# One offset for layer 1's weight halves, eight-wide inverse roots on GpSimd, and a planner with other costs

## The chip, the cores and the metric

The kernel runs on one core of a Trainium2 chip. The metric is device time in microseconds (us) of one execution; before the change the median of three runs is 1524.97 us (1524.93 to 1526.73). All numbers are float32; products run in the `float32r` form of TensorE unless said otherwise.

## The reference

Two layers over 256 latent and 256 context tokens of width 1024. Cut to what matters:

```python
for l in range(2):
    mod = silu(c) @ w_mod[l] + b_mod[l]           # and the same for c_ctx
    h = rms_norm(x, norm1_g[l]) * (1 + sc1) + sh1
    z = h @ w_in[l]                               # 14 column groups
    y_da  = differential attention, heads rms-normed before and after
    y_gla = chunked gated linear attention, both directions, rms-normed heads
    y_na  = 2-D neighbourhood attention
    m = sum over the three of sigmoid(gate) * (y @ w_br)
    x = x + g1 * (m @ w_out)
    h2 = rms_norm(x, norm2_g[l]) * (1 + sc2) + sh2
    x = x + g2 * (relu(h2 @ w_ff1) ** 2 @ w_ff2)
```

In layer 0 latent and context tokens go through everything (512 columns). In layer 1 the context only feeds keys, values and states, so most products have 256 columns. Every `rms_norm` needs `1 / sqrt(mean + eps)`: of 2 or 4 values per partition for the layer norms and the attention's output heads, of 8 for the linear attention's heads, of 16 or 32 for queries and keys. The linear attention's decay needs `gla_a2`, `gla_a_b` (in the kernel one array, `gl`: the gate factors) and triangular matrices (`tri`).

## The kernel before, in words

**Weights.** All weights stream once, as 290 pieces of 128 x 1024 float32 (512 KB, `raw`, 5 buffers), 145 a layer, over SP's DMA queue. Each piece is split into a rounded half and a rest: ScalarE copies it into `wh`, VectorE subtracts into `wl` (128 x 1152 tiles of which 1024 columns are used, 5 buffers each). A product is three matmuls: `wh` with the high half of the data, `wh` with the low half, `wl` with the high half. In `tok_job` (the token-major projections) the weights are the moving operand and 512 wide; in `chan_mm` (gates, branches, output projection, both MLP products) the weights are the stationary operand, 128 x 128, and the data moves, 512 columns in layer 0 and 256 in layer 1.

**Where a piece lies.** A `wh` or `wl` tile is 1152 x 4 = 4608 bytes, nine times 512, per partition. Pieces of layer 0 and of the token-major projections start at its begin. Layer 1's other pieces are planned with `shift=True`; `split_weights` takes their columns from an offset that depends on the place in the turn of five:

```python
SHIFTS = 16, 48, 64, 80, 112
i = SHIFTS[st["ring"]] if plan[n][1] else 0
st["ring"] = (st["ring"] + 1) % NW
h, lo = [buf(t, t, 1152, NW, F32R)[:, i:i + 1024] for t in ("wh", "wl")]
```

These are 64, 192, 256, 320 and 448 bytes. Piece n, counted from 0, has place n mod 5; the last one, 289, has place 4.

**The order of the work.** It is written by a planner while the program is built. Generators (the stream of projections `stream`, `branches` with the three attentions, `norms`, `mods_task`, `begin`) yield a time at which they could go on; `drive` takes the next that is ready, or the earliest. Times come from `Plan.note`, which adds up costs per engine from the tables `FIXED`, `PER`, `SLOWER`, `SWITCH` and `LATENCY`. `refill` adds a split of a piece when the planned time of its load has come. `copy` and `square` choose ScalarE or VectorE by `act_first`. Each engine then runs its own queue strictly in the order written, so an instruction that waits holds back all behind it on that engine.

**Inverse roots.** `rsqrt` is a seed from the bits and three Newton steps, all on VectorE: a scaling with eps, one seed, and 9 small instructions. `norm_rms` (6 calls) runs it for the layer norms and copies the result into `rb`, which TensorE broadcasts (`norm_bcast`); `heads_rms` runs it for queries and keys (8 calls on 16 or 32 values) and for the linear attention (3 on 8 values); `head_end` in `da_attn` for the output heads (8 on 2 or 4 values). The result is 8192 times the negative root; the constant `RS` takes that back.

**Gate factors and triangles.** The job `ga` in `start` issues `sb` and the two `gl` tiles on SP's queue (both 128 x 512), multiplies the decay's input, splits the second `gl` tile into `a2s` during the product, and evicts the product as `gat`. The linear attention's first products (`la`) need `a2s` and `gat`. The triangles `tri` are loaded as `trif` from ScalarE's queue and cast on VectorE at the end of `first_norm`, just ahead of the cast of the masks (`mskf` to `msk`).

Of the kernel before, what the change touches and what calls it, by code (L numbers as in the profile page):

```python
# [19 lines left out]
P = 128  # L20
D = 1024
# [15 lines left out]
OFF_GATE = (4640, 5664, 6688)  # L37


RS = -1.0 / 8192.0  # L40

SA_BMOD, SA_N1, SA_N2, SA_W = 0, 48, 56, 64
SB_GQ, SB_GQP, SB_GK, SB_GKP = 0, 64, 128, 192
# [8 lines left out]
DA_K, NA_K = 4, 4  # L52
ACT_BIAS, NORM_LATE = 0.3, (5.0, 2.0, 2.0, 5.0)
HOLD = 0
SHIFTS = 16, 48, 64, 80, 112
STAT_PAD = 0.0

SWITCH, SLOWER = 0.095, {1: 1.057, 2: 1.0, 4: 1.03}
FW = -1
REFINE = True  # L60
AHEAD = 2
# [7 lines left out]
MOD1_AFTER = (0, "ff1", 0)  # L69


FIXED = {"DVE": 0.068, "ACT": 0.1, "Pool": 0.045, "PE": 0.005}
PER = {"DVE": 1.04e-3, "ACT": 0.833e-3, "Pool": 2.3e-3, "PE": 1 / 2400}
LATENCY = {"DVE": 0.13, "ACT": 0.2, "Pool": 0.13, "PE": 0.25, "DMA": 2.0}
DMA_PER_BYTE = 2.9 / 2 ** 20


class Plan:
# [13 lines left out]
    def note(self, lane, op, args, kw):  # L92
        aps = [x for x in args[1:] if isinstance(x, bass.AP)]
        aps += [v for k, v in kw.items() if isinstance(v, bass.AP) and k != "accum_out"]
        out = args[0]
        width = lambda x: math.prod(x.shape[1:])
        n = width(out)
        if op == "dma_start":
            us = n * out.shape[0] * 4 * DMA_PER_BYTE
            self.now["DMA"] = max(self.now["DMA"], self.now["PE"]) + us  # L100
            self.wr[out.tensor.name] = max(self.now["DMA"], self.rd.get(out.tensor.name, 0.0) + us) + LATENCY["DMA"]
            return
        if lane == "PE":
            passes = 2 if op == "transpose" else 1 if aps[0].dtype == F32R else 4
            us = max(n, 64) * passes * PER["PE"] * out.shape[0] * aps[0].shape[0] / P ** 2 * SLOWER[passes] + FIXED["PE"]
            shape = aps[0].shape[0], out.shape[0]
            kind = shape, passes
            us += SWITCH * (shape != self.kind[0]) + SWITCH * (kind != self.kind and kind == ((P, P), 1))
            self.kind = kind
        else:  # L110
            n = max(n, max((width(x) for x in aps), default=0))
            sb = lane == "DVE" and op in ("tensor_copy", "tensor_scalar", "memset") and \
                not any(x.tensor.name.startswith("ps") for x in aps)
            us = FIXED[lane] + n * PER[lane] * (0.5 if sb else 1)
            pointers = sum(width(x) == 1 for x in aps) if n > 1 else 0
            if lane == "ACT" and REFINE:
                us += 0.09 * (pointers + ("accum_out" in kw)) - (0.042 if aps[0].tensor.name.startswith("ps") else 0)
            elif lane == "ACT" and "accum_out" in kw:
                us += 0.09
            elif lane == "DVE" and REFINE and pointers:  # L120
                us += 0.06
        start = max(self.now[lane], self.ready(aps), self.rd.get(out.tensor.name, 0.0))
        end = start + us
        self.now[lane] = end
        for x in aps:
            self.rd[x.tensor.name] = max(self.rd.get(x.tensor.name, 0.0), end)
        for x in [out] + ([kw["accum_out"]] if "accum_out" in kw else []):
            self.wr[x.tensor.name] = end + LATENCY[lane]

# [30 lines left out]
def build(nc, tc, ctx, a):  # L160
# [63 lines left out]
    def after(key):  # L224
        return lambda: 0.0 if key in done else INF
# [23 lines left out]
        else:  # L249
            V.tensor_tensor(out, x, x, MULT)  # L250

    def rsqrt(dst, x, tmp):

        V.tensor_scalar(dst.bitcast(I32), x.bitcast(I32), -0.5, 1597463007.0, MULT, ADD)
        n = x.shape[-1]
        for thr in (3.0, 12.0, 768.0):
            if n <= 2:
                for i in range(n):
                    c = slice(i, i + 1)
                    V.scalar_tensor_tensor(tmp[:, c], dst[:, c], dst[:, c], x[:, c], MULT, MULT)  # L260
            else:
                V.tensor_tensor(tmp, dst, dst, MULT)
                V.tensor_tensor(tmp, tmp, x, MULT)
            V.scalar_tensor_tensor(dst, tmp, -thr, dst, ADD, MULT)

    plan = []
    st = {"load": 0, "split": 0, "cur": 0, "more": 0, "raw": 0, "room": 0, "hold": 0, "ring": 0}
    raws, parts, held = {}, {}, []  # L270

    def plan_w(src, width=2048, shift=False):
# [10 lines left out]
    def split_weights(force=False):  # L283
# [14 lines left out]
        if held[-1]:  # L298
            w = []
            for c in cs:  # L300
                w.append((u("xw", dtype=F32R), u("xw", dtype=F32R)))
                S.activation(w[-1][0], s[:, c], AF.Copy)
                V.tensor_tensor(w[-1][1], s[:, c], w[-1][0].bitcast(F32), SUB)
        else:

            i = SHIFTS[st["ring"]] if plan[n][1] else 0
            st["ring"] = (st["ring"] + 1) % NW
            h, lo = [buf(t, t, 1152, NW, F32R)[:, i:i + 1024] for t in ("wh", "wl")]
            S.activation(h, s, AF.Copy)
            V.tensor_tensor(lo, s, h.bitcast(F32), SUB)  # L310
            w = [(h[:, c], lo[:, c]) for c in cs]
# [82 lines left out]
    V.memset(ones, 1.0)  # L394
    rope = const("rope", [P, 2, 2, HD])
    tri = const("tri", [P, 4, P], F32R)
    ind = const("ind", [P, P])
    msk = const("msk", [P, 2, 4, P], U8)
    cc = const("cc", [P, KT, 2])
# [3 lines left out]
    m01 = const("m01", [P, KT, 2, 2])  # L403
    mod[0][0], mod[0][1] = m01[:, :, 0], m01[:, :, 1]
    scl = [[const(f"scl{l}{n}", [P, KT, 2]) for n in range(2)] for l in range(DEPTH)]


    def mod_scale(l, n, k0, k1, ns=2):
# [74 lines left out]
    def norm_rms(ps, nt):  # L483

        ms = small("ms", [P, 4])
        V.tensor_scalar(ms[:, :nt], ps.rearrange("p (t c) -> p t c", c=P)[:, :nt, 0], 1.0 / D, EPS, MULT, ADD)
        r = small("nr", [P, 4])
        tmp = small("nt", [P, 4])
        rsqrt(r[:, :nt], ms[:, :nt], tmp[:, :nt])
        rb = u("rb").rearrange("p (t c) -> p t c", c=P)  # L490
        V.tensor_copy(rb[:, :nt], r[:, :nt].unsqueeze(2).to_broadcast([P, nt, P]))
        return rb
# [117 lines left out]
    def heads_rms(zs, width):  # L610
# [6 lines left out]
            S.activation(sq, z, AF.Square)  # L617
            V.tensor_reduce(ss[:, i * g:(i + 1) * g], sq.rearrange("p (g w) -> p g w", w=width), AX.X, ADD)
        yield need(ss, lane="DVE")
        V.tensor_scalar(ss, ss, 1.0 / width, EPS, MULT, ADD)  # L620
        r = small(f"sr{n * g}", [P, n * g])
        tmp = small(f"st{n * g}", [P, n * g])
        rsqrt(r, ss, tmp)
        return r.rearrange("p (n g) -> p n g", g=g)

    def scale_heads(out, z, r, width):
# [84 lines left out]
    def da_attn(L, lam_init, y):  # L711
# [103 lines left out]
        def head_end(h, left):  # L815
# [5 lines left out]
                yield need(o[t], lane="ACT")  # L821
                S.activation(sq[:, t * P:(t + 1) * P], o[t][:, c], AF.Square, accum_out=ss[:, t:t + 1])
            yield need(ss, lane="DVE")
            V.tensor_scalar(ss, ss, 1.0 / P, EPS, MULT, ADD)
            rsqrt(r, ss, tmp)
            for t in range(0, nq, 2):
                for s_ in (t, t + 1):
                    copy(o[s_][:, c], o[s_][:, c], r[:, s_:s_ + 1])
# [110 lines left out]
    def gla(L, y):  # L939
# [21 lines left out]
        for t in (2, 3, 0, 1):  # L961
            las[t] = split(la[t])

        yield after((l, "gv"))
        am0 = [u("amask") for _ in range(2)]
        for t in am0:
# [124 lines left out]
    def start(l, h):  # L1091
# [25 lines left out]
        def ga():  # L1117
# [1 line left out]
            SP.dma_start(L["sb"], a["sb"][l])  # L1119
            ab, a2 = u("gl"), u("gl")  # L1120
            for i, t in enumerate((ab, a2)):
                SP.dma_start(t, a["gl"][l, i])

            a2s = u("a2", dtype=F32R)[0:96]
            L["gl"] = ab, a2s
# [397 lines left out]
    def first_norm():  # L1523
# [15 lines left out]
        yield from norm_apply(0, 0, x0, pb, 0, NTOK, NTOK, h, [0, 1], ready)  # L1539
        for dst, n in ((ind, "ind"), (rope, "rope")):  # L1540
            S.dma_start(dst, a[n])
        trif = u("trif").rearrange("p (r c) -> p r c", r=4)
        S.dma_start(trif, a["tri"])
        V.tensor_copy(tri, trif)
        mskf = u("mskf")[:, :2 * P].rearrange("p (r c) -> p r c", r=2)
        S.dma_start(mskf, a["msk"].rearrange("p (r c) -> p r c", r=2))
        for r in range(2):
# [136 lines left out]
```

## Time and profile before

| | us |
|---|---|
| median of three runs | 1524.97 |
| the profiled execution | 1523.46 |
| its span | 1521.3 |
| TensorE busy in it | 1487.3 |
| VectorE busy | 1068.6 |
| ScalarE busy | 707.2 |
| GpSimd busy | 20.8 |

The profiled execution took 1523.46 us, 2.2 us more than its span, and 1.5 us less than the median of the runs. "PE" is TensorE, "DVE" VectorE, "ACT" ScalarE, "POOL" GpSimd, "SP" the engine that issues most DMAs. In the profile all the kernel's recorded operations stand under one line (L141, the recording call), so they are told apart by the tiles' names. `psg` are accumulators of the projections, `pss` those of attention and norms. The record of one matmul lasts longer than the pitch at which matmuls follow each other; pitches are taken here from start times or from windows with a known number of matmuls.

### The profile page before, as it was taken

The numbers are of one execution on the slowest core, as the hardware profiler recorded it, in microseconds if no ns is written. First come the engines' busy times: TensorE is split into PE (matmuls) and PEld (weight loads), VectorE is DVE, ScalarE is ACT, GpSimd is POOL, SyncE is SP. The second block draws the span as 40 slices with busy tenths as digits, with TensorE's granted clock in tenths as the row PEclk, the third lists the DMA queues.
The fourth block names the chain that finished last, engine by engine and source line by source line (L and its number), as shares of the span: only waits on it lengthen the run. The fifth ranks groups of instructions, "written<-read, shape, count | busy, mean of one in ns | idle before, by whom it ended". The sixth has DMA issues, their size and how long they took to land.

```text
span 1521.3 us, 24039 instructions
## 1 busy us (share of the span) xinstructions
PE 1487.3 (98%) x9340; PEld 1279.3 (84%) x9340; DVE 1068.6 (70%) x2242; ACT 707.2 (46%) x1243; POOL 20.8 (1%) x30
## 2 busy tenths in 40 slices
PE   7899999999999999999999999999999999999999
PEld 5788878888877888988888888888887889989999
DVE  5788796698986376698876334877867685786543
ACT  4444435553345433623324252464466455477632
POOL 0100000000000100100000000000000000000000
PEclk9999999999999999999999999999999999999999
DMA  9533331157522422366885222324224325346662
GB/s 364 189 108 104 97 112 56 56 187 224 185 80 67 139 97 84 132 219 199 262 274 173 97 97 91 111 70 133 84 77 138 130 92 186 128 164 202 208 201 78
DMA packets 77793, 216.66 MB, mean 142 GB/s; under 512 B 9072, under 2 KB 12528, under 8 KB 77680
## 3 DMA queue, kind: packets, MB, share of 16 engines
q1 hardware_dynamic: 74880, 210.28, 41.7%
q10 hardware_dynamic: 2160, 2.76, 0.6%
q0 software_dynamic: 640, 2.10, 0.4%
q8 instruction: 73, 1.20, 0.3%
q14 instruction: 40, 0.33, 0.1%
HBM read 214.05 MB, written 1.05 MB: 141 GB/s over the span
## 4 chain that ended last, share of the span: by engine, by line
PE 75%; DVE 17%; ACT 3%; DMA 3%; issue 2%; SPq 0%; ACTq 0%; DVEq 0%
PE psg L141 63%; PE pss L141 11%; DVE wl L141 4%; DVE dump L141 2%; DVE z L141 2%; DVE wm L141 2%; DMA wm<-w_mod 2%; ACT wh L141 1%; DVE ss L141 1%; DMA gl<-gl 1%; DVE hn L141 1%; DVE h L141 1%; DVE S L141 1%; DVE st L141 0%; DMA raw<-w_tok 0%
## 5 line engine op out<-in xcount | busy, mean ns | idle before, releaser
L141 DVE TENSOR_TENSOR wl<-raw,wh 128x1024 fp32r<-128x1024 f32 x290 | 354.2, 1228 | 163.1 <-ACT wh L141 162.7
L141 PE MATMUL psg<-h,wh 128*128 128x256 f32 (+1 forms) x1808 | 444.4, 337 | 3.9 <-ACT z L141 2.0
L141 ACT ACTIVATE wh<-raw 128x1024 fp32r<-128x1024 f32 x290 | 301.7, 1053 | 195.3 <-PE psg L141 186.2
L141 PEld LDWEIGHTS psg<-h,wh 128*128 128x128 f32 x1808 | 305.6, 190 | 43.6 <-issue 5.5
L141 PE MATMUL psg<-wh,h 128*128 128x512 f32 (+1 forms) x1056 | 333.3, 391 | 0.1
L141 PE MATMUL psg<-h,wl 128*128 128x256 f32 (+1 forms) x904 | 301.4, 333 | 0.5 <-DVE wl L141 0.5
L141 PE MATMUL psg<-act,wh 128*128 128x256 f32 (+1 forms) x1056 | 249.0, 329 | 0.0
L141 PEld LDWEIGHTS psg<-wh,h 128*128 128x128 f32 x1056 | 197.7, 188 | 43.9 <-issue 2.5
L141 PE MATMUL psg<-wl,h 128*128 128x512 f32 (+1 forms) x528 | 204.3, 387 | 0.0
L141 PEld LDWEIGHTS psg<-act,wh 128*128 128x128 f32 x1056 | 178.3, 188 | 18.8
L141 PEld LDWEIGHTS psg<-h,wl 128*128 128x128 f32 x904 | 171.1, 189 | 18.1 <-DVE wl L141 0.8
L141 PE MATMUL psg<-act,wl 128*128 128x256 f32 (+1 forms) x528 | 173.9, 329 | 0.0
L141 DVE SCALAR_TENSOR_TENSOR dump<-wm,cb 128x512 f32<-128x512 f32 x160 | 107.8, 686 | 19.4 <-DMA wm<-w_mod 17.0
L141 PEld LDWEIGHTS psg<-wl,h 128*128 128x128 f32 x528 | 99.6, 189 | 18.9
L141 PEld LDWEIGHTS psg<-act,wl 128*128 128x128 f32 x528 | 99.4, 188 | 9.4
L141 PE MATMUL psg<-y,wh 128*128 128x512 f32 (+1 forms) x384 | 96.4, 342 | 0.0
L141 DVE TENSOR_TENSOR act<-r,act 128x256 fp32r<-128x256 f32 (+1 forms) x65 | 36.2, 557 | 66.9 <-ACT act L141 66.9
L141 DVE SCALAR_TENSOR_TENSOR x<-psg,mod,x 128x256 f32<-128x256 f32 x96 | 43.1, 479 | 56.7 <-PE psg L141 56.7
L141 ACT ACTIVATE r<-psg 128x256 f32<-128x256 f32 (+1 forms) x63 | 30.0, 476 | 95.8 <-PE psg L141 95.8
L141 PEld LDWEIGHTS psg<-y,wh 128*128 128x128 f32 x384 | 64.3, 189 | 7.3 <-issue 0.7
L141 PE MATMUL psg<-sp,wh 128*128 128x256 f32 (+1 forms) x304 | 66.5, 315 | 1.7 <-ACT sp L141 1.4
L141 DVE SCALAR_TENSOR_TENSOR wm<-wm,cb 128x512 f32<-128x512 f32 x96 | 66.2, 690 | 2.7
(223 smaller groups left out, 1679.4 us busy)
## 6 DMA issues: line engine op xcount, KB each, us to landing
raw<-w_ff SPq DMA_DIRECT2D x128, 512.0 KB, 4.4
wm<-w_mod SPq DMA_DIRECT2D x192, 256.0 KB, 4.0
raw<-w_tok SPq DMA_DIRECT2D x72, 512.0 KB, 4.0
raw<-w_gate SPq DMA_DIRECT2D x48, 512.0 KB, 3.9
raw<-w_br SPq DMA_DIRECT2D x24, 512.0 KB, 3.5
raw<-w_out SPq DMA_DIRECT2D x16, 512.0 KB, 3.8
tb<-natb SPq DMA_DIRECT2D x16, 192.0 KB, 4.1
x<-xc SPq DMA_DIRECT2D x8, 256.0 KB, 4.1
```

Of the source, the lines that this page charges most:

```text
L141: r = f(*args, **kw)
```

## The change

- `SHIFTS` becomes one number: all shifted pieces of layer 1 start 16 values (64 bytes) into their tile.
- `rsqrt` becomes `inv_rms`. Up to 8 values: VectorE scales (by `RS * RS`, so that the result is 8192 times the root), and GpSimd raises to -0.5 in one `tensor_tensor` with `ALU.pow`. These are 17 calls: 6 of `norm_rms`, 3 of the linear attention, 8 of `head_end`. Above 8 values the Newton steps stay on VectorE. The sign of the result is now positive, in the seed as well, and `RS` with it.
- The `gl` loads are issued from ScalarE's queue instead of SP's.
- `tri` is cast in `gla` of layer 0, after the splits of the decay, by `copy`.
- The planner's numbers change: a load is taken to arrive 3.3 after its transfer instead of 2.0; a matmul costs a little less, the slower kinds a little more; `pow` has a price of its own.

```diff
-RS = -1.0 / 8192.0
+RS = 1.0 / 8192.0
-SHIFTS = 16, 48, 64, 80, 112
+SHIFT = 16
-SWITCH, SLOWER = 0.095, {1: 1.057, 2: 1.0, 4: 1.03}
+SWITCH, SLOWER = 0.095, {1: 1.0622, 2: 1.01, 4: 1.05}
-FIXED = {"DVE": 0.068, "ACT": 0.1, "Pool": 0.045, "PE": 0.005}
+FIXED = {"DVE": 0.068, "ACT": 0.1, "Pool": 0.045, "PE": 0.0006}
-LATENCY = {"DVE": 0.13, "ACT": 0.2, "Pool": 0.13, "PE": 0.25, "DMA": 2.0}
+LATENCY = {"DVE": 0.13, "ACT": 0.2, "Pool": 0.13, "PE": 0.25, "DMA": 3.3}
...
+            if ALU.pow in args:
+                us = 0.35 + 0.185 * n
...
+    def inv_rms(dst, x, n, tmp, src=None):
+        src = x if src is None else src
+        m = x.shape[-1]
+        if m <= 8:
+            V.tensor_scalar(x, src, RS * RS / n, RS * RS * EPS, MULT, ADD)
+            G.tensor_tensor(dst, x, nhalf[:, :m], ALU.pow)
+            return
+        V.tensor_scalar(x, src, 1.0 / n, EPS, MULT, ADD)
...
-            i = SHIFTS[st["ring"]] if plan[n][1] else 0
-            st["ring"] = (st["ring"] + 1) % NW
+            i = SHIFT if plan[n][1] else 0
...
+        if l == 0:
+            copy(tri, trif[0])
         yield after((l, "gv"))
...
-                SP.dma_start(t, a["gl"][l, i])
+                S.dma_start(t, a["gl"][l, i])
...
-        V.tensor_copy(tri, trif)
```

What moves, at three places. First ScalarE's queue in layer 0 at the gate factors (`z` are evictions of the first projection, `wh` a weight split, `a` is `a2s`), before and then with the change:

```order
L141 ACTIVATE z_641<-psg_372 128x512
L141 ACTIVATE z_648<-psg_376 128x512
L141 ACTIVATE wh_665<-raw_336 128x1024
L141 ACTIVATE a_153_656<-gl_653 96x512
L141 ACTIVATE gat_708<-psg_671 96x512
L141 ACTIVATE wh_725<-raw_395 128x1024
```

```order
L143 ACTIVATE z_639<-psg_354 128x512
L143 ACTIVATE z_644<-psg_358 128x512
L143 DMA gl_648<-gl 128x512
L143 DMA gl_649<-gl 128x512
L143 ACTIVATE wh_665<-raw_377 128x1024
L143 ACTIVATE a_155_652<-gl_649 96x512
L143 ACTIVATE gat_701<-psg_661 96x512
```

The two loads now stand behind the last `z`, and `a2s` still follows the next `wh`. Second TensorE's queue at the same place, where the products of the decay (`a`, `gat`) stand between products of the next projection, before and then with the change:

```order
L141 MATMUL psg_735<-wh_599,h_303 128x512
L141 MATMUL psg_735<-wl_600,h_303 128x512
L141 MATMUL psg_735<-wh_599,h_304 128x512
L141 MATMUL pss_739<-a_153_656,gat_708 128x512
L141 MATMUL pss_744<-a_153_656,gat_708 128x512
```

```order
L143 MATMUL psg_722<-wh_591,h_285 128x512
L143 MATMUL psg_731<-wh_591,h_284 128x512
L143 MATMUL psg_731<-wl_592,h_284 128x512
L143 MATMUL psg_731<-wh_591,h_285 128x512
L143 MATMUL pss_735<-a_155_652,gat_701 128x512
```

One more group of three 512-column matmuls stands ahead of the decay's products (four groups instead of three; the same in layer 1). Third VectorE's queue at the first half of layer 0's second norm (`ms` the mean, `nr` and `nt` the Newton steps, `rb` the copy that TensorE broadcasts), before and then with the change:

```order
L141 TENSOR_SCALAR ms_5849<-pss_5844 128x2
L141 TENSOR_SCALAR nr_5851<-ms_5849 128x2
L141 SCALAR_TENSOR_TENSOR nt_5852<-nr_5851,ms_5849 128x1 x2
L141 SCALAR_TENSOR_TENSOR nr_5851<-nt_5852,nr_5851 128x2
...
L141 COPY rb_5863<-nr_5851 128x256
L141 SCALAR_TENSOR_TENSOR x_5542<-psg_5831,mod_87,x_5542 128x256
L141 TENSOR_TENSOR sq_5581<-sq_5581,sq_5878 128x256
L141 TENSOR_TENSOR wl_5900<-raw_5642,wh_5899 128x1024
```

```order
L143 TENSOR_SCALAR ms_5788<-pss_5783 128x2
L143 COPY rb_5793<-nr_5789 128x256
L143 SCALAR_TENSOR_TENSOR x_5481<-psg_5770,mod_89,x_5481 128x256
L143 TENSOR_TENSOR sq_5520<-sq_5520,sq_5808 128x256
L143 TENSOR_TENSOR wl_5824<-raw_5581,wh_5823 128x1024
```

Nothing stands between `ms` and `rb` on VectorE any more; the root `nr` is GpSimd's.

## Rows read from the trace of the kernel before

**Rows 1.** The page, busy time of each engine
```profile
PE 1487.3 (98%) x9340; PEld 1279.3 (84%) x9340; DVE 1068.6 (70%) x2242; ACT 707.2 (46%) x1243; POOL 20.8 (1%) x30
```

**Rows 2.** The chain that ended last: start us, us, what
```profile
1349.96 168.21 PE psg L141 x1442
```

**Rows 3.** Windows over five successive pieces of layer 1: length, busy per engine, clock, DMA
```profile
1350.31:1353.04 2.73, 2.73 (x26) 2.73 (x25) 2.67 (x3) 2.66 (x6) 0.00 (x0) 1.00 0.09 26
1353.04:1355.76 2.72, 2.72 (x26) 2.72 (x25) 2.35 (x4) 2.42 (x5) 0.00 (x0) 1.00 0.92 303
1355.76:1358.63 2.88, 2.88 (x26) 2.88 (x25) 1.74 (x9) 1.72 (x5) 0.00 (x0) 1.00 0.93 272
1358.63:1361.47 2.83, 2.83 (x26) 2.83 (x25) 2.07 (x6) 2.83 (x8) 0.00 (x0) 1.00 0.40 155
1361.47:1364.29 2.82, 2.82 (x26) 2.82 (x25) 2.10 (x3) 2.73 (x7) 0.00 (x0) 1.00 0.08 20
```

**Rows 4.** Timeline of PE in layer 0, output projection, 256 columns
```profile
593.33 0.40 PE L141 MATMUL psg<-sp,wh 128*128 128x256 f32 x2
593.69 0.40 PE L141 MATMUL psg<-sp,wh 128*128 128x256 f32 x2
```

**Rows 5.** Groups by form, PE, 990 to 1521 us: xcount | busy us, mean ns
```profile
L141 PE MATMUL psg<-h,wh 128*128 128x256 f32 x848 | 154.7, 283 | 1.2 <-DVE h L141 1.0
...
L141 PE MATMUL psg<-act,wl 128*128 128x256 f32 x256 | 71.5, 279 | 0.0
```

**Rows 6.** What PE waited for: us in total, times, longest
```profile
PE pss L141 <- DVE sq L141: 6.1, 1, 6.1
...
PE pss L141 <- DVE gat L141: 3.0, 2, 2.2
...
PE pss L141 <- ACT dao L141: 1.3, 2, 0.9
...
PE pss L141 <- DVE rb L141: 0.6, 1, 0.6
...
PE pss L141 <- ACT kd L141: 0.3, 1, 0.3
```

**Rows 7.** Windows around two falls of the clock, columns as in rows 3
```profile
52.50:65.07 12.57, 8.37 (x36) 6.29 (x36) 8.03 (x18) 6.21 (x10) 4.49 (x6) 1.00 0.79 277
65.07:68.48 3.41, 3.41 (x9) 2.67 (x10) 3.31 (x5) 0.63 (x1) 0.00 (x0) 0.50 0.36 102
...
600.97:607.79 6.82, 6.33 (x28) 6.04 (x29) 6.54 (x20) 2.04 (x4) 0.00 (x0) 0.50 0.48 156
```

**Rows 8.** Timelines in layer 0 at the gate factors: DVE, ACT, SP, PE
```profile
50.77 0.43 DVE L141 CAST tri<-trif 128x512 fp32r<-128x512 f32 x1 [2.93 <-DMA trif<-tri]
...
54.33 2.04 ACT L141 ACTIVATE z<-psg 128x512 f32<-128x512 f32 x4
...
56.10 0.88 SPq L141 DMA_DIRECT2D gl<-gl  x2
...
62.06 0.63 ACT L141 ACTIVATE a<-gl 96x512 fp32r<-96x512 f32 x1 [4.74 <-DMA gl<-gl]
...
64.91 1.95 PE L141 MATMUL pss<-a,gat 96*128 96x512 f32 x4 [2.17 <-DVE gat L141]
```

**Rows 9.** Timeline of PE in layer 1 at the gate factors
```profile
983.45 1.20 PE L141 MATMUL pss<-a,gat 96*128 96x512 f32 x4 [0.80 <-DVE gat L141]
```

**Rows 10.** Timeline of a norm's root in layer 1: DVE, then PE
```profile
962.06 0.15 DVE L141 TENSOR_SCALAR ms<-pss 128x2 f32<-128x2 f32 x1
...
964.54 0.71 PE L141 MATMUL pss<-ident,rb 128*128 128x128 f32 x4 [0.57 <-DVE rb L141]
```

**Rows 11.** GpSimd's multiplications; VectorE beside GpSimd; VectorE's group of splits
```profile
344.78 2.54 POOL L141 TENSOR_TENSOR cb<-cb,cbt 128x512 f32<-128x512 f32 x2 [285.87 <-DVE cbt L141]
...
638.87 2.31 DVE L141 TENSOR_TENSOR wl<-raw,wh 128x1024 fp32r<-128x1024 f32 x1
...
L141 DVE TENSOR_TENSOR wl<-raw,wh 128x1024 fp32r<-128x1024 f32 x290 | 354.2, 1228 | 163.1 <-ACT wh L141 162.7
```

More of the change, by code (lines that the diff above doesn't have):

```diff
@@ L250, in square @@
             V.tensor_tensor(out, x, x, MULT)
-    def rsqrt(dst, x, tmp):
-        V.tensor_scalar(dst.bitcast(I32), x.bitcast(I32), -0.5, 1597463007.0, MULT, ADD)
-        n = x.shape[-1]
-        for thr in (3.0, 12.0, 768.0):
[L257 to L263, printed above, removed]
+    def inv_rms(dst, x, n, tmp, src=None):
[6 more added lines that the diff above has]
+        V.tensor_scalar(x, src, 1.0 / n, EPS, MULT, ADD)
+        V.tensor_scalar(dst.bitcast(I32), x.bitcast(I32), -0.5, 1597463007.0 - 2.0 ** 31, MULT, ADD)
+        for thr in (3.0, 12.0, 768.0):
+            V.tensor_tensor(tmp, dst, dst, MULT)
+            V.tensor_tensor(tmp, tmp, x, MULT)
             V.scalar_tensor_tensor(dst, tmp, -thr, dst, ADD, MULT)
     plan = []
-    st = {"load": 0, "split": 0, "cur": 0, "more": 0, "raw": 0, "room": 0, "hold": 0, "ring": 0}
+    st = {"load": 0, "split": 0, "cur": 0, "more": 0, "raw": 0, "room": 0, "hold": 0}
     raws, parts, held = {}, {}, []
@@ L396, in build @@
     tri = const("tri", [P, 4, P], F32R)
+    nhalf = const("nhalf", [P, 8])
+    V.memset(nhalf, -0.5)
     ind = const("ind", [P, P])
@@ L405, in build @@
     scl = [[const(f"scl{l}{n}", [P, KT, 2]) for n in range(2)] for l in range(DEPTH)]
+    trif = []
     def mod_scale(l, n, k0, k1, ns=2):
@@ L485, in norm_rms @@
         ms = small("ms", [P, 4])
-        V.tensor_scalar(ms[:, :nt], ps.rearrange("p (t c) -> p t c", c=P)[:, :nt, 0], 1.0 / D, EPS, MULT, ADD)
         r = small("nr", [P, 4])
         tmp = small("nt", [P, 4])
-        rsqrt(r[:, :nt], ms[:, :nt], tmp[:, :nt])
+        inv_rms(r[:, :nt], ms[:, :nt], D, tmp[:, :nt], ps.rearrange("p (t c) -> p t c", c=P)[:, :nt, 0])
         rb = u("rb").rearrange("p (t c) -> p t c", c=P)
@@ L619, in heads_rms @@
         yield need(ss, lane="DVE")
-        V.tensor_scalar(ss, ss, 1.0 / width, EPS, MULT, ADD)
         r = small(f"sr{n * g}", [P, n * g])
         tmp = small(f"st{n * g}", [P, n * g])
-        rsqrt(r, ss, tmp)
+        inv_rms(r, ss, width, tmp)
         return r.rearrange("p (n g) -> p n g", g=g)
@@ L823, in head_end @@
             yield need(ss, lane="DVE")
-            V.tensor_scalar(ss, ss, 1.0 / P, EPS, MULT, ADD)
-            rsqrt(r, ss, tmp)
+            inv_rms(r, ss, P, tmp)
             for t in range(0, nq, 2):
@@ L1541, in first_norm @@
             S.dma_start(dst, a[n])
-        trif = u("trif").rearrange("p (r c) -> p r c", r=4)
-        S.dma_start(trif, a["tri"])
-        V.tensor_copy(tri, trif)
+        trif.append(u("trif").rearrange("p (r c) -> p r c", r=4))
+        S.dma_start(trif[0], a["tri"])
         mskf = u("mskf")[:, :2 * P].rearrange("p (r c) -> p r c", r=2)
```

## The prediction

> **What bounds the kernel.** I read the page's busy times first: TensorE is busy 98% of the span, VectorE 70%, ScalarE 46% [rows 1]. So time can only come from two places: TensorE's own pace, and the moments in which it waits. The list of what TensorE waited for has 18 lines, from 6.1 us down to 0.3, together 30.1 us [rows 6]; more than that no repair of waits can give, but for one thing beside it. After some waits the granted clock falls: after the waits of 52.5 to 65.07 us the records show 3.41 us at 0.50, the lower of the two levels (1.2 instead of 2.4 GHz), and again 6.82 us at 600.97 [rows 7]. At half clock half of the stretch is lost, 1.7 and 3.4 us.
>
> The pace is read from the chain of waits and from windows. From 1349.96 us to the end the chain is nothing but projections, 1442 matmuls in 168.21 us, 116.65 ns each [rows 2]. That is not one pace. I cut this stretch at every 24th matmul, which is one weight piece: the same work takes 2.73, 2.72, 2.88, 2.83 and 2.82 us, at full clock and with TensorE never idle [rows 3]. The five together, 13.98 us, are one turn of the buffers. Counted back from the end (1349.96 + 168.21 = 1518.17) the fifth window lies 153.9 / 13.98 = 11.0 turns ahead of the last piece, which has place 4; so the windows are places 0 to 4, with offsets of 64, 192, 256, 320 and 448 bytes. Pieces at 64 and 192 run at 113.5 ns a matmul, at 256 at 120, at 320 and 448 at 118.
>
> **The offsets.** The change gives all five places 64 bytes. The tile is nine times 512 bytes long, so the offset within 512 bytes is then the same in every buffer. That this offset counts and not the buffer, I take from layer 0, where pieces lie at offset 0: its 256-column matmuls come three in 0.36 us, 120 ns [rows 4], like the piece at 256 bytes. What it touches: 24 gate, 12 branch, 8 output and 64 MLP pieces of layer 1, 108 x 24 = 2592 matmuls (the groups of 848 and 256 are among them [rows 5]). At 13.98 / 120 = 116.5 ns now and 113.5 then this is 3.0 ns x 2592 = 7.8 us. In the last 168 us and most of layer 1 nothing else is on the path, so it counts in full. VectorE and ScalarE do 10.93 and 12.37 us of work in these 13.98 us (the windows' sums [rows 3]), so they keep up with 13.6. Ends: 0, if the offset is not the cause; 8.2 us with the chain's mean (116.65) and the faster window.
>
> The Trainium skill's "TensorE: Matmul & The Clock Gate", section on the back-to-back issue gap, makes the gap a matter of columns alone, an estimate of 256 / 2.4 + 2.5 = 109 ns, and "SBUF — State Buffer", section "SBUF: two separate sides", says that TensorE never waits for anyone there. By these the offset would be worth nothing. The windows disagree: 24 equal matmuls differ by 0.16 us with their place.
>
> **Gate factors.** In layer 0 TensorE waits 2.17 us at 64.91 for `gat`, whose chain starts with the `gl` loads: issued on SP at 56.10, used on ScalarE at 62.06 after it had stood idle 4.74 us [rows 8]. With the change ScalarE issues them behind its four `z` (54.33 to 56.4 [rows 8]), thus no earlier; but they are not behind a weight piece and four `w_mod` tiles on SP's queue any more. And three more matmuls of 512 columns stand ahead of the decay's products, some 0.68 us of cover. I take 0.7 for the cover and 0.5 for the landing, 1.2 in all (ends 0 and 2.17), and 0.5 for the clock's stretch behind it (0 to 1.7: the wait just ahead of it, for ScalarE's `z`, stays, as `z` still stand behind the tanh that waits for `cb`). ScalarE pays two issues, about 0.9 us, in a place where it was idle. In layer 1 the wait is 0.80 us [rows 9]: the same group of three ahead covers 0.68, I take 0.5 (0 to 0.8).
>
> **Triangles.** VectorE stood 2.93 us for `trif` at 50.77 [rows 8]. The next instruction casts the masks, whose load was issued right behind on the same queue; that wait takes its place. The cast itself, 0.43 us, goes to ScalarE after the decay's splits. Behind it on VectorE is a weight split that TensorE doesn't reach before 60 us. Worth 0; ends 0 and 0.4.
>
> **Inverse roots.** A root on VectorE with its hand-over to TensorE takes 964.54 - 962.06 = 2.48 us, of which TensorE waited 0.57 [rows 10]; its other work covers 1.9. The change leaves 0.15 for the scaling and about 0.3 for the copy on VectorE, adds two hand-overs (some 0.3, an estimate) and the power p on GpSimd. No row shows a power. From below it is nearly nothing; from above I set 2.5, twice the nearest row, a multiplication of 512 columns in 2.54 / 2 = 1.27 us [rows 11]. I take 1.0, near that row and under it since only 2 to 8 columns go through. The chain is then 1.75, under the cover, and the 0.57 goes; in the output heads TensorE waited 1.3 us in two places [rows 6], of which I count nothing. So 0.6; ends 1.9 gained (0.6 + 1.3), or at p = 2.5 five norms (the first hides behind the loads) later by 3.25 - 1.9, 6.8 us lost. The copy `rb` now waits at VectorE's head for GpSimd, with residuals and a weight split behind it; at present VectorE computes in that time, so nothing behind it comes later unless p passes 1.6. VectorE is relieved of 17 x about 1.9 = 32 us at most, which is not on the path.
>
> There is a price on the other side. GpSimd's multiplications stretched a split beside them from 1.228 to 2.31 us [rows 11]. The Trainium skill's "SBUF — State Buffer", section "SBUF: two separate sides", has the reason: GpSimd and a VectorE instruction with two SBUF inputs exclude each other for an instruction's length. By it each of the 17 powers could hold a split back by p, 17 us of VectorE at 1.0, half of the relief. The row agrees.
>
> **The rest of the order.** The planner's other costs shift splits by a place or two everywhere. The largest waits have their causes left in place: the root's input `sq` (6.1 us), and in layer 1 a split that still stands ahead of the last gate product. I count 0, with 6 us to either side.
>
> **Sum.** 7.8 + 1.2 + 0.5 + 0.5 + 0.6 = 10.6 us. The profiled execution took 1523.46 us: 1512.9. The median of the runs stands 1.5 above it, so 1514.
>
> **Rivals.**
> - The pace comes, the waits come back. The new order makes TensorE wait in three new places for about 2 us each, each followed by half clock as in rows 7: 3 x (2 + 1.7) = 11 us, less what overlaps with waits now there: about 1523. For it: waits sum to 30 us and the order was redone for all. Against: the places that I compared keep their sequence. Chance 0.10, half of it no change, the rest to both sides.
> - The offset is not the cause (the skill's rule above): the pace belongs to a buffer or to what else runs beside that piece. Then the 7.8 falls away: 1522. For it: in layer 1 each offset has had one buffer only. Against: two windows at 113.5 and layer 0's 120. Chance 0.05, mostly no change.
> - The power is slow, and the time ends on the other side. At p = 4 us the chain of five norms is 4.75 against a cover of 1.9, 2.85 x 5 = 14 us, each with half clock behind it (1.7 x 5 = 8.5): 1514 + 22 = 1536. It decides from p of about 2.5. For it: no row shows the operation. Against: the nearest operation takes 1.27. Chance 0.03.
> - The new order removes more waits than counted: 8 us more, 1506. Chance 0.04.
>
> **The numbers.** The forecast has 0.78, by itself 1508 to 1519. A difference under 0.2% (3 us) can't be told from none. Faster: 0.78 + 0.04 + parts of the first two rivals, 0.87; same 0.08; slower 0.05. The range goes from the last rival's side, 1506, to 1521, where most of the first two lies beyond.
>
> **What would show it.** Five successive pieces near the end alike at 2.72 us, and the last stretch at about 113.5 ns a matmul; if two or three places stay at 2.82 to 2.88, the offset isn't it. At the gate factors a wait of TensorE of about 1 us in layer 0 and under 0.4 in layer 1, with the loads issued on ScalarE's queue at about 56 us. VectorE still idle for `mskf` where it waited for `trif`. The power near 1 us and no wait for `rb` above 0.3. The forecast is wrong if the pace doesn't change, or if the list of waits grows by more than 6 us.

## The result and the profile after

The changed kernel takes 1512.55 us (median of 5 runs, 1510.38 to 1516.65) against 1524.97: a ratio of 0.9925 (0.9904 to 0.9946), 12.4 us less. 1514 had been forecast, so the number was right. The reason was not: the largest term, 7.8 us for TensorE's pace in layer 1, is zero in the trace after. In that execution two terms that the forecast priced at 0.5 and 0.6 us made up for it, stretches at half clock and the roots; over the runs only the gain at the roots holds.

The page of the changed kernel, busy time of each engine (answers to [rows 1]):

```profile
PE 1478.1 (98%) x9340; PEld 1275.1 (84%) x9340; DVE 1037.9 (69%) x2072; ACT 708.5 (47%) x1244; POOL 38.3 (3%) x47
```

VectorE has 170 instructions and 31 us less, GpSimd 17 instructions and 17.5 us more. The chain that ended last has the same 1442 projections at its end as in [rows 2] (start, length, what):

```profile
1336.85 170.12 PE psg L143 x1442
```

That is 118.0 ns each, against 116.65: the last stretch has become slower by 1.9 us. The windows (columns as in [rows 3]) are two successive pieces of 24 matmuls at 1266 us and two at 1343 us, all at 64 bytes, and the window of the only fall of the clock inside the work:

```profile
1265.94:1268.66 2.72, 2.72 (x27) 2.72 (x25) 0.94 (x1) 1.55 (x2) 0.00 (x0) 1.00 0.61 215
1268.66:1271.38 2.72, 2.72 (x27) 2.72 (x25) 1.51 (x2) 1.06 (x1) 0.00 (x0) 1.00 0.48 154
1342.82:1345.65 2.83, 2.83 (x26) 2.83 (x25) 2.18 (x8) 1.65 (x5) 0.00 (x0) 1.00 0.78 258
1345.65:1348.48 2.83, 2.83 (x26) 2.83 (x25) 2.15 (x7) 2.83 (x8) 0.00 (x0) 1.00 0.47 156
...
1297.90:1301.31 3.41, 3.41 (x18) 3.41 (x18) 2.96 (x5) 1.54 (x3) 0.00 (x0) 0.50 0.29 91
```

The five places are alike now, but at either of two paces: 2.72 / 24 = 113.3 ns from 1250 to about 1331 us, waits and the half clock apart, and 2.83 / 24 = 117.8 ns for every piece from 1337 us to the end. And in this execution the clock fell once (3.41 us at 0.50) where it had fallen four times, 17.1 us in all, before [rows 7].

What TensorE waited for (us, times, longest; the list has 18 lines and 28.7 us, against 30.1 in [rows 6]):

```profile
PE pss L143 <- DVE sq L143: 6.4, 1, 6.4
PE psg L143 <- DVE gat L143: 3.7, 2, 2.4
PE psg L143 <- ACT z L143: 3.0, 2, 1.8
PE pss L143 <- DVE e L143: 2.1, 1, 2.1
...
PE pss L143 <- DVE z L143: 1.2, 2, 0.6
...
PE pss L143 <- ACT kd L143: 0.3, 1, 0.3
```

`rb` and `dao` have left the list. The gate factors (`gat`) have not: 3.7 us where there were 3.0. The timelines there, first in layer 0 (VectorE, ScalarE with its queue, TensorE; answer to [rows 8]), then in layer 1 (the same engines; answer to [rows 9]):

```profile
49.59 0.76 DVE L143 CAST msk<-mskf 128x512 uint8<-128x512 f32 x2 [3.40 <-DMA mskf<-msk]
...
52.01 0.82 ACTq L143 DMA_DIRECT2D gl<-gl  x2
52.50 2.05 ACT L143 ACTIVATE z<-psg 128x512 f32<-128x512 f32 x4
...
58.95 0.63 ACT L143 ACTIVATE a<-gl 96x512 fp32r<-96x512 f32 x1 [3.46 <-DMA gl<-gl]
...
59.73 0.69 DVE L143 SCALAR_TENSOR_TENSOR dump<-wm,cb 128x512 f32<-128x512 f32 x1 [2.96 <-DMA wm<-w_mod]
...
61.89 0.68 DVE L143 TENSOR_TENSOR a<-gl,a 32x512 fp32r<-32x512 f32 x1
62.60 0.68 DVE L143 TENSOR_TENSOR gat<-psg,gat 32x512 fp32r<-32x512 f32 x1
...
63.34 0.50 PE L143 MATMUL psg<-wh,h 128*128 128x512 f32 x1 [2.44 <-DVE gat L143]
```

```profile
973.64 0.68 DVE L143 TENSOR_TENSOR a<-gl,a 32x512 fp32r<-32x512 f32 x1 [2.17 <-ACT a L143]
974.36 0.68 DVE L143 TENSOR_TENSOR gat<-psg,gat 32x512 fp32r<-32x512 f32 x1
...
966.36 1.61 ACTq L143 DMA_DIRECT2D gl<-gl  x2
...
972.98 0.63 ACT L143 ACTIVATE a<-gl 96x512 fp32r<-96x512 f32 x1 [2.95 <-DMA gl<-gl]
...
975.09 0.50 PE L143 MATMUL psg<-wh,h 128*128 128x512 f32 x1 [1.27 <-DVE gat L143]
```

In layer 0 the loads go out 2.26 us earlier, counted from the start of `z` (before: 1.77 behind it; now 0.49 ahead, although they stand behind `z` in the queue), and ScalarE still waits 3.46 us for them. When its part is done at 60.06, VectorE is in the middle of the modulation's products (`dump`, `wm`), for which it had itself waited 2.96 us; `a` and `gat` stand behind them, and TensorE waits 2.44 us instead of 2.17. In layer 1 VectorE is not the cause: it idles 2.17 us for ScalarE's `a`, and that waits for the loads until 972.98, 6.62 us after their issue began. Before the change it was 981.33 - 976.17 = 5.16 us:

```profile
976.17 0.90 SPq L141 DMA_DIRECT2D gl<-gl  x2
...
981.33 0.63 ACT L141 ACTIVATE a<-gl 96x512 fp32r<-96x512 f32 x1 [3.88 <-DMA gl<-gl]
```

In both layers the matmul that waits is now a `psg` one: the first of the group of three that was moved ahead of the decay's products. The kernel has four `psg` accumulators (`BANKS = (4, 4)`). The gate product holds one until `gat` is read from it, and the three groups behind it take the others, so the fourth group has to wait for `gat` as well and covers nothing.

A root in layer 1 (VectorE, GpSimd, VectorE, TensorE; answers to [rows 10]):

```profile
943.40 0.16 DVE L143 TENSOR_SCALAR ms<-pss 128x2 f32<-128x2 f32 x1 [2.04 <-PE pss L143]
943.71 0.70 POOL L143 TENSOR_TENSOR nr<-ms,nhalf 128x2 f32<-128x2 f32 x1 [309.60 <-DVE ms L143]
944.44 0.29 DVE L143 COPY rb<-nr 128x256 f32<-128x256 f32 x1 [0.88 <-POOL nr L143]
945.00 0.61 PE L143 MATMUL pss<-ident,rb 128*128 128x128 f32 x4
```

945.00 - 943.40 = 1.60 us at most, where it was 2.48, and TensorE does not wait. GpSimd's groups by form give the power's price:

```profile
L143 POOL TENSOR_TENSOR sr<-ss,nhalf 128x8 f32<-128x8 f32 x3 | 6.4, 2149 | 184.1 <-DVE ss L143 184.1
L143 POOL TENSOR_TENSOR der<-des,nhalf 128x4 f32<-128x4 f32 x4 | 4.0, 1007 | 144.0 <-ACT pt L143 113.4 <-DVE des L143 30.5
L143 POOL TENSOR_TENSOR nr<-ms,nhalf 128x2 f32<-128x2 f32 x5 | 3.5, 700 | 580.1 <-DVE ms L143 580.1
```

0.70 us for 2 columns, 1.01 for 4, 2.15 for 8 (1.95, 2.01 and 2.49).

To see where time goes over a whole execution, I took from each trace the distance from every matmul's start to the next, put it down to the first of the two, and sorted it (us; L1 256: what exceeds 113.3 ns in layer 1's 256-column matmuls that are not waiting; half clock: half of the time at 0.50; small: all the time of the matmuls into `pss`, waits behind them included; large: what waits add behind matmuls into `psg`; head: up to the first matmul; what is left over is within 1 us of before):

| kernel | L1 256 | half clock | small | large | head | span |
|---|---|---|---|---|---|---|
| before | 7.8 | 8.5 | 225.5 | 33.6 | 6.1 | 1521.3 |
| changed | 7.8 | 1.7 | 219.3 | 35.1 | 6.4 | 1510.1 |
| a0_again | 8.2 | 8.5 | 220.4 | 34.5 | 7.5 | 1518.6 |
| a1_rotation | 7.7 | 5.1 | 218.4 | 34.0 | 7.2 | 1512.1 |
| a2_before_64 | 1.7 | 8.5 | 225.7 | 34.9 | 6.3 | 1516.9 |
| b1_reset | 2.0 | 5.1 | 218.8 | 34.5 | 6.5 | 1506.7 |
| c1_costs | 7.9 | 12.0 | 225.1 | 33.1 | 6.3 | 1523.4 |
| c2_roots | 8.0 | 1.7 | 219.5 | 32.8 | 6.5 | 1508.4 |
| d1_order | 8.4 | 3.4 | 225.9 | 42.8 | 6.6 | 1527.0 |
| d2_root | 8.1 | 5.1 | 223.7 | 31.1 | 8.2 | 1516.2 |
| e1_best | 1.7 | 3.4 | 219.9 | 32.8 | 6.1 | 1503.7 |

The column of small matmuls lies some 3 us above the plain sum, by the same amount in every row, so its differences count. Before to changed: pace 0, half clock -6.8, small matmuls -6.2, large +1.5, head +0.3.

### The profile page after: what moved, and what is told of

The parts are those of the page before. It is cut to its first block, busy times and chain, and to the rows that moved or that the text cites. A ratio compares the mean times of both kernels' runs of the same rounds, so it can differ in the third digit from the quotient of the medians.

```text
span 1510.1 us, 23888 instructions
## 1 busy us (share of the span) xinstructions
PE 1478.1 (98%) x9340; PEld 1275.1 (84%) x9340; DVE 1037.9 (69%) x2072; ACT 708.5 (47%) x1244; POOL 38.3 (3%) x47
## 5 line engine op out<-in xcount | busy, mean ns | idle before, releaser
L143 ACT ACTIVATE r<-psg 128x256 f32<-128x256 f32 (+1 forms) x63 | 30.1, 477 | 95.6 <-PE psg L143 90.4
```

The source lines that it names most:

```text
L143: r = f(*args, **kw)
```

## The experiments

**The changed kernel again (a0_again).** No edit.

> The changed kernel as it is, profiled once more. In its first trace the 256-column matmuls of layer 1, all at 64 bytes, ran at 113.3 ns a matmul from 1250 to 1331 us, whatever the place, and at 117.8 ns from 1337 us to the end (1442 matmuls in 170.1 us). Theory A (the offset alone sets the pace, and something else slowed the last stretch in that one execution): the last stretch comes out near 113.5 ns, 163.7 us. Theory B (at 64 bytes two paces are possible, and what TensorE did on entering a stretch chooses one, which it then keeps): the last stretch is wholly at 113.3 (163.4 us) or wholly at 117.8 (170 us); if the choice is a matter of chance it may differ from the first trace. Theory C (the order of the kernel's instructions fixes it): 170.1 us again, stretch by stretch as before. The number of stretches at half clock, 1 in the first trace against 4 of the kernel before, may differ too: the granted clock of the five runs was 0.995 to 0.999. Time 1512 +- 3.

1510.99 us (1507.48 to 1520.33), ratio 0.9928 (0.9900 to 0.9956). The chain's last piece:

```profile
1345.26 170.12 PE psg L143 x1442
```

170.12 again, so A falls. But the executions are not alike. Taking (1 - granted clock) x span off each of the 11 runs of this kernel leaves 1501.5 to 1513.6 us, with four from 1501.5 to 1502.8, two at 1505.0 and 1506.5, and five from 1508.5 to 1513.6: about the 6.4 us between a last stretch at 113.3 and one at 117.8. That is B, with chance in it; all but two of these runs have no trace, so it is only likely. C falls with `b2_all64` below: every engine has the same order there, only layer 0's offsets differ, and the last stretch takes 163.72 us. And the clock fell four times here, 17.1 us as in the kernel before: the single fall of the first trace does not repeat.

**Old offsets in the new order (a1_rotation).**
```diff
-            i = SHIFT if plan[n][1] else 0
+            i = SHIFTS[st["ring"]] if plan[n][1] else 0
+            st["ring"] = (st["ring"] + 1) % NW
```

> The changed kernel, with the old offsets back (64, 192, 256, 320, 448 bytes by place); its order of instructions is the same on every engine. Theory A (64 bytes gives 113.5 ns and the rotation 116.5): 2592 matmuls x 3.0 ns = 7.8 us slower than the changed kernel, 1520. Theory B (64 bytes alone is 113.3 or 117.8 by stretch, on average as good as the rotation): places 0 and 1 at 113.3, place 2 at 119.9, places 3 and 4 at 118; last stretch 168.2 us against 170.1, so the whole time within 2 us of the changed kernel, 1511 to 1514.

1512.13 us, ratio 0.9924 (0.9905 to 0.9943): as fast as with 64 bytes. Last stretch 168.21 us as in [rows 2], and with the clock taken off the five runs stand within 0.9 us. Theory B.

**64 bytes in the old order (a2_before_64).**
```diff
-SHIFTS = 16, 48, 64, 80, 112
+SHIFTS = 16, 16, 16, 16, 16
```

> The kernel before, with 64 bytes at all five places; its order of instructions is unchanged. Theory A: 7.8 us faster than before, 1517, all pieces of the last stretch at 113.5. Theory B: each stretch of layer 1 settles at 113.3 or 117.8; the last one at 163.4 us (then about 1517) or at 170 us (then 1524 to 1527). If the whole gain of the change lies in its order, this kernel stays within 0.2% of the kernel before when the last stretch settles at 117.8.

1523.20 us, ratio 0.9997 (0.9981 to 1.0012): the offsets alone change nothing in the median. Yet in this trace the last stretch is fast:

```profile
1349.99 163.73 PE psg L141 x1442
```

163.73 is 113.5 ns, what the prediction expected, and its 12 runs go from 1517.52 to 1529.35, wider than 17 runs of the kernel before (1518.53 to 1526.87). It is likely, but not shown without traces of them, that 64 bytes draws between a better and a worse pace than the rotation's mixture.

**Other offsets (a3_map).**
```diff
+SHIFTS = 8, 24, 32, 40, 96
```

> The changed kernel with other offsets by place: 32, 96, 128, 160 and 384 bytes; the order of instructions unchanged. Theory A: each place has a pace of its own, some of the five near 113.3 and some near 118 to 120, the same in every turn of the last stretch. Theory B: the pace of a place depends on the one ahead of it: a place that can be fast is fast when it follows a fast one or one like 448 bytes. No number is forecast for the single offsets; multiples of 128 bytes are thought nearer to 120 (as 0 and 256 are), the others nearer to 113.3.

1516.88 us in one run, last stretch 171.66. Two of the five places of one turn, by windows:

```profile
1354.89:1357.73 2.84, 2.84 (x26) 2.84 (x25) 2.32 (x4) 2.74 (x7) 0.00 (x0) 1.00 0.73 238
...
1363.42:1366.31 2.89, 2.89 (x26) 2.89 (x25) 1.70 (x3) 2.17 (x4) 0.00 (x0) 1.00 0.68 238
```

The other three take 2.84 and 2.85: at 32, 96, 128, 160 and 384 bytes all places are slow (118.3 to 120.4 ns), 32 and 96 against my guess. The offset does count; of those tried only 64, 192, 320 and 448, the odd multiples of 64, ran at 113.3 in any trace.

**Four places at 64, one at 448 (b1_reset).**
```diff
+SHIFTS = 16, 16, 16, 16, 112
```

> The changed kernel with offsets of 64 bytes at places 0 to 3 and 448 at place 4; its order of instructions is unchanged. Theory B1 (a run of equal pieces keeps the pace it came in with, and the step from 448 back to 64 bytes always starts the fast one, as it does in every turn of the rotation): a slow pace lasts a turn at most, after that places 0 to 3 stand at 113.3; place 4 at 113.3 if it follows a fast piece, else 117.7. Last stretch 163.4 to 164.7 us instead of 168.2 with the rotation and 170 at 64 alone; the time 3 to 5 us under the rotation's: 1507 to 1509. Theory B2 (the rotation's step at 256 bytes is what resets): the last stretch keeps 117.8 at all five places, 170 us, and the time is 1512 to 1514.

1509.05 us, ratio 0.9906 (0.9889 to 0.9922). The last stretch:

```profile
1339.80 163.71 PE psg L143 x1442
```

With the clock taken off, the six runs lie at 1501.9 to 1504.2, where a1_rotation's lie at 1508.6 to 1509.5; the ratios as measured (a1_rotation: 0.9905 to 0.9943) overlap. The mechanism of B1 is not confirmed, though: from 1305 us on this trace has six slow pieces in a row, across a step from 448 to 64.

**Layer 0 at 64 bytes too (b2_all64).**
```diff
-            i = SHIFT if plan[n][1] else 0
+            i = SHIFT
```

> The changed kernel, with layer 0's weight pieces at 64 bytes as well (in the changed kernel they start at 0); its order of instructions is unchanged. If the offset counts for 512 columns too, layer 0's 512-column matmuls fall from 226.7 ns to about 220 in those where the weights stand still or move at 64 bytes: 3960 x 6.7 = up to 26 us. If it counts for 256 columns alone: 512 columns stay at 226.7, layer 0's 256-column ones may go from 120 to 113.3 or 117.8, at most 380 x 6.7 = 2.5 us.

1522.71 us in one run, 10 slower than the changed kernel, with layer 1's last stretch at 163.72. Matmuls of 512 columns get slower: start to start they exceed 226.7 ns by 19.3 us in sum, against 2.1 in the changed kernel. 64 bytes has nothing to give for 512 columns; no other offset was tried there.

**Planner costs alone (c1_costs).**
```diff
-SWITCH, SLOWER = 0.095, {1: 1.057, 2: 1.0, 4: 1.03}
+SWITCH, SLOWER = 0.095, {1: 1.0622, 2: 1.01, 4: 1.05}
-... "PE": 0.005} ... "DMA": 2.0}
+... "PE": 0.0006} ... "DMA": 3.3}
```

> The kernel before with the changed planner costs alone (the table of shares for slower engines, TensorE's fixed cost, 3.3 instead of 2.0 us for a load): offsets rotate, roots on VectorE, gate factors on SyncE's queue, the triangle's cast in its old place. Theory D1 (the gain of about 12 us is the planner's): 1513 to 1518, with TensorE's time in small matmuls down from 225.5 to about 219 us and fewer stretches at half clock. Theory D2 (the gain comes from the roots on GpSimd and the chains that they shorten): 1522 to 1528, no gain from the costs alone.

1522.36 us, ratio 0.9989 (0.9976 to 1.0002): no measurable gain, small matmuls at 225.1 us. D1 falls. The costs do move something: with the clock taken off the median is 1512.8, against 1516.4 for the kernel before beside it, but the granted clock averages 0.9939 against 0.9955, which takes most of that back.

**Roots alone (c2_roots).** The changed kernel with old costs, old offsets, `gl` on SyncE's queue and the old triangle cast; only `inv_rms`, with the planner's price for the power, is new.

> The kernel before with the roots on GpSimd alone (old costs, old offsets, gate factors on SyncE's queue, the triangle's cast in its old place). Theory D1: 1522 to 1528, only the waits for rb and the root's z go, under 2 us. Theory D2: 1513 to 1518, small matmuls down from 225.5 to about 219 us.

1512.16 us, ratio 0.9931 (0.9915 to 0.9948): this one part gives the whole gain. `gat` waits 2.6 us here, less than with the loads on ScalarE. Its granted clock was 0.999 in four of six runs, 0.9978 on average; in the runs of the kernel before it averaged 0.9955. With the clock taken off, the medians are 1510.4 and 1516.4.

**New order, old roots (d1_order).** Does the root itself gain, or the order that the planner makes of its cost? Here the planner books the power, and VectorE executes the old root.
```diff
-            V.tensor_scalar(x, src, RS * RS / n, RS * RS * EPS, MULT, ADD)
-            G.tensor_tensor(dst, x, nhalf[:, :m], ALU.pow)
+            pl.note("DVE", "tensor_scalar", (x, src, ...), {})
+            pl.note("Pool", "tensor_tensor", (dst, x, nhalf[:, :m], ALU.pow), {})
+            ...  # the old root, called on V.engine, so not booked
```

> The order that the planner chose with the roots on GpSimd (that of the run with the roots alone), on every engine, but with the roots themselves executed on VectorE as in the kernel before: VectorE's 1.9 us a root stand in the place of scaling, power and hand-over, and the planner is told the costs of the power. Offsets rotate, costs old. Theory E1 (the gain comes from the roots themselves: a shorter chain, VectorE relieved of 30 us): the gain is gone, 1521 to 1526. Theory E2 (the gain comes from the order that the planner makes out of the changed costs): it stays, 1510 to 1515, with TensorE's time in small matmuls near 220 us. Theory E3 (both are needed): 1515 to 1520.

1528.69 us, ratio 1.0040 (1.0025 to 1.0055): slower than before. The list of waits names the roots' readers:

```profile
PE pss L143 <- DVE rb L143: 4.4, 5, 1.0
PE pss L143 <- ACT dao L143: 3.6, 4, 1.4
...
PE pss L143 <- DVE go L143: 1.8, 1, 1.8
```

E2 falls: without the short root the order that was planned for it costs 5.2 us.

**Old order, new roots (d2_root).** The counterpart: the power is executed, the old root's costs are booked, and TensorE, ScalarE and SyncE have the instructions of the kernel before in the same order.

> The counterpart: the order of the kernel before on TensorE, ScalarE and SyncE, instruction for instruction, with the 17 roots of up to 8 columns executed as a power on GpSimd; the planner is told the old costs. Theory E1: the gain is there without a new order, 1510 to 1515. Theory E2: 1521 to 1526; only the waits for rb (0.6 us) and the last head's (1.3 us) go. Theory E3: 1515 to 1521.

1515.81 us, ratio 0.9951 (0.9933 to 0.9969). The waits for `rb` and `dao` are gone, that for `z` at about 432 us is still there:

```profile
PE pss L143 <- DVE z L143: 3.8, 6, 1.4
```

So the roots by themselves are worth 7.6 us, and none of the three theories was quite right: this run lies between E1 and E3, d1_order above the ranges of all. In the order that the planner then finds, that of c2_roots, the `z` waits fall to 1.2 us, but whether this adds to the gain is not shown: the ratios of the two runs overlap (0.9915 to 0.9948 and 0.9933 to 0.9969), and with the clock taken off their medians are 1510.4 and 1511.3.

TensorE runs the same 9340 matmuls in the same order here as in the kernel before, so the two traces can be laid side by side. d2_root's first matmul starts 2.1 us later and its last 5.1 us earlier, 7.3 us gained. Of these 1.8 lie at the matmuls that read `rb` and 1.7 at those that read `dao`, and 3.4 in stretches at half clock. The last part is not shown to hang on the roots. The kernel before falls to half clock behind a wait of 2.06 us for `e`; d2_root has the same wait and no fall (each wait, then the window behind it):

```profile
1115.28 0.63 PE L141 MATMUL pss<-ident,e 128*128 128x128 f32 x4 [2.06 <-DVE e L141]
1116.40:1119.80 3.40, 3.40 (x15) 2.43 (x14) 2.05 (x2) 2.54 (x5) 0.00 (x0) 0.50 0.56 175
...
1113.33 0.63 PE L143 MATMUL pss<-ident,e 128*128 128x128 f32 x4 [2.06 <-DVE e L143]
1114.45:1117.85 3.40, 3.40 (x27) 2.85 (x26) 2.05 (x2) 2.54 (x5) 0.00 (x0) 1.00 0.60 175
```

**Roots with 64, 64, 64, 64, 448 (e1_best).** The edit is to c2_roots.
```diff
-SHIFTS = 16, 48, 64, 80, 112
+SHIFTS = 16, 16, 16, 16, 112
```

> The kernel before with the roots on GpSimd and offsets of 64 bytes at places 0 to 3, 448 at place 4. By the runs so far: roots alone 1512.2 with the rotation; the same offsets took 6.2 us out of the last stretch and the time of the changed kernel's order, at the same clock. Theory B1 (448 to 64 starts the fast pace at the head of the last stretch): last stretch 163.4 us, the time 1505 to 1508, faster than both kernels. Theory B2 (chance): last stretch at 163.4 or 170 us, the five times spread over 7 us, median 1506 to 1513.

1506.74 us (1505.46 to 1507.50), ratio 0.9890 (0.9870 to 0.9910), last stretch 163.73: faster than both kernels, 5.4 us under the same kernel with the rotation, whose ratio (0.9915 to 0.9948) lies clear of this one.

**Roots with 64, 64, 64, 64, 256 (e2_256).**
```diff
+SHIFTS = 16, 16, 16, 16, 64
```

> The same as the kernel before with the roots on GpSimd, offsets 64 bytes at places 0 to 3 and 256 at place 4. A piece at 256 bytes runs at 120 ns in every turn. Theory B2 (the step away from 256 bytes decides the pace anew): in the rotation the piece behind 256 bytes comes out at 118.0, so places 0 to 3 may stand at 118 in every turn, last stretch 170 us, 1514. Theory B1': behind 256 bytes the pace at 64 is 113.3 in every turn: last stretch 165.3 us, about 1509. A mixture by turns would show that neither holds.

1515.76 us, ratio 0.9951 (0.9937 to 0.9966). Windows over places 3, 4 (256 bytes) and 0 in the first turn of the last stretch:

```profile
1347.37:1350.09 2.72, 2.72 (x26) 2.72 (x25) 2.24 (x8) 2.72 (x8) 0.00 (x0) 1.00 0.54 196
1350.09:1352.97 2.88, 2.88 (x26) 2.88 (x25) 1.88 (x3) 2.79 (x7) 0.00 (x0) 1.00 0.03 7
1352.97:1355.80 2.83, 2.83 (x26) 2.83 (x25) 2.31 (x3) 2.73 (x6) 0.00 (x0) 1.00 0.70 236
```

The stretch comes in fast; the first piece at 256 bytes takes 120 ns, and from there to the end no piece at 64 is fast again (170.34 us). That is the clearest row of the study: at the same offset and in the same buffer a piece runs at either pace (place 3 at 113.3 ns here, at 117.8 in all later turns). At 1256 us of this trace, as at 1350, TensorE came to a piece at 256 bytes at the fast pace and left it at the slow one without a wait, so what ran ahead counts. But 256 bytes doesn't always bring the slow pace. In the kernel before a piece at 320 bytes ran fast right behind one at 256 (places 2 and 3; the data changes from `y` to `h` between them):

```profile
1260.60:1263.50 2.90, 2.90 (x27) 2.90 (x26) 1.16 (x2) 2.49 (x3) 0.00 (x0) 1.00 0.57 195
1263.50:1266.22 2.72, 2.72 (x27) 2.72 (x26) 2.60 (x5) 1.06 (x1) 0.00 (x0) 1.00 0.50 163
```

## Why the prediction was right and wrong

**The offsets, -7.8: wrong.** The step that failed is "the offset within 512 bytes is then the same in every buffer", hence one pace, 113.5 ns. The runs showed two at 64 bytes, 113.3 and 117.8 ns, and what exceeds 113.3 ns in layer 1 sums to 7.8 us before and after. The windows of [rows 3] did show a pace by place, but I read each place's pace as its own, when it was also what the place ahead had left: places 0 and 1 are fast *within the rotation*. The warning was in the trace: earlier in layer 1, from 1092 to 1097 us, places 0 and 1 of the kernel before run at 117.8:

```profile
1092.00:1094.83 2.83, 2.83 (x26) 2.83 (x25) 2.73 (x6) 0.68 (x2) 0.00 (x0) 1.00 0.54 182
1094.83:1097.65 2.82, 2.82 (x27) 2.82 (x26) 2.72 (x6) 0.00 (x0) 0.00 (x0) 1.00 0.01 3
```

I read the last stretch alone, and did not ask whether the same offset was fast everywhere. In the medians 64 bytes is worth nothing that can be told: a2_before_64 0.9997, and a1_rotation, which takes it back, stays at 0.9924. The rival (offset not the cause, 0.05) was not right either: offsets do change the pace (a3_map, e2_256), and with it the time (e1_best against c2_roots), but what ran ahead does so too. What sets the pace on entering a stretch was not settled, nor why 448 in the fifth place kept the last stretch fast in all that was seen of b1_reset and e1_best: both their traces, and ten runs within 3.3 us with the clock taken off.

**Inverse roots, -0.6: the mechanism was right, the size wrong by about ten times.** The power costs 0.70 for 2 columns (I took 1.0), the chain 1.6 (I took 1.75). The step that failed is "and the 0.57 goes" as the price of the norms' roots, and "of which I count nothing" for the heads. d2_root, with TensorE's order fixed, shows what it is worth: 7.6 us in the medians, and 5.4 with the clock taken off (1511.3 against 1516.7). Laid side by side, the traces show 3.5 us at the readers of `rb` and `dao`, where the list of waits has 0.6 and 1.3 and I counted 0.6 in all. I had taken the chain's listed wait for its price, and had put the heads at nothing without a reason. Of the rest, the wait for `z` ahead of the gate products falls from 2.0 to 1.3, and one stretch at half clock goes and one is halved; that the short root does this is not shown (the wait for `e` above, and d1_order's granted clock, which averages 0.9976 with the old roots). Nor do the runs part the shorter chain from VectorE's relief, which I had called "not on the path": both come with the power. What the planner's order adds, which I had put at 0 with 6 to either side, is not told from nothing.

**The price at GpSimd: not paid.** What the prediction drew from the Trainium skill ("SBUF — State Buffer", section "SBUF: two separate sides"), that a power could hold a split back by its whole length, does not show. Of the changed kernel's 17 powers 14 have no VectorE instruction beside them: VectorE waits for their results. The best case is in c2_roots, where a split starts 0.37 us into a power and both take their usual time (VectorE, then GpSimd; the group's mean for a split is 1.227 us there):

```profile
115.90 1.23 DVE L143 TENSOR_TENSOR wl<-raw,wh 128x1024 fp32r<-128x1024 f32 x1
...
115.53 1.95 POOL L143 TENSOR_TENSOR sr<-ss,nhalf 128x8 f32<-128x8 f32 x1 [58.25 <-DVE ss L143]
```

Only a power that starts during a split is longer, by 0.5 us; that split takes 1.218 us.

**Clock, -0.5: 6.8 in the trace, much less in the runs.** The granted clock averaged 0.9957 over the changed kernel's 11 runs and 0.9953 over the 53 of the kernel before, so this part of the profiled gain does not hold over the runs. What stands in its place there is at most in part the offset: with the clock taken off, the median is 1506.5 for the changed kernel and 1509.1 for a1_rotation, 2.6 us apart, but the former's 11 runs scatter over 12 us, and the medians as measured side by side (1510.99 and 1512.13) differ by 1.1: a1_rotation's granted clock averages 0.9978. How the 12.4 us of the medians divide beyond the roots stays open to that extent.

**Gate factors, -1.2 and -0.5: wrong.** +0.3 in layer 0; in layer 1 1.27 instead of 0.80 [rows 9]. The step that failed is "some 0.68 us of cover": the group that was to cover the wait needs the accumulator that `gat` frees, and waits with it. "Thus no earlier" failed too, as the loads went out ahead of `z` in layer 0; what stands ahead of `a` and `gat` on VectorE used that up. In layer 1 the loads landed later after their issue than from SP's queue; why is open.

**Triangles, 0: right**, as forecast: VectorE waits 3.40 us for `mskf` in place of 2.93 for `trif`.

**The sum** held by luck: 7.8 not gained stood against some 11 gained at the roots. By its own test ("wrong if the pace doesn't change") the explanation failed.

## What to carry to other kernels

A short chain that stands in front of the busiest engine many times can be worth more than its listed waits: here 1.9 us in the list were 3.5 us of TensorE's time, and the medians moved by more. To price such a chain, change it alone, hold the order of the busiest engine, and lay the two traces side by side. An order planned for the cheap form and run with the dear one lost 5.2 us, so the planner's costs have to be those that run. Before a per-place pace is taken as a property of the place, look for the same place in another sequence: one counter-example in the trace of before would have done. And when a forecast's total comes out, undo its largest term: here it was worth nothing.

## What the runs showed of the hardware that was not expected

- 256-column matmuls with stationary pieces at 64 bytes run for hundreds of matmuls at 113.3 or at 117.8 ns, at full clock and with TensorE never idle. In e2_256's last stretch the first piece at 256 bytes (120 ns) turned 113.3 into 117.8, which stayed to the end; in the kernel before one such piece was followed by 113.5. 512-column matmuls lose by the same offset (226.7 ns at 0, 229 to 236 in b2_all64, one run).
- A power on GpSimd takes 0.70, 1.01 and 1.95 to 2.01 us for 2, 4 and 8 columns; 2.49 where it starts during a split with two SBUF inputs. The splits beside a power did not slow down (1.218 to 1.227 us).
- The granted clock fell once in one execution of the changed kernel and four times in another, and the same 2.06 us wait was followed by half clock in one kernel and not in the other.
